# A hybrid decoder layer on one core: pinned even mix in the middle stage, and a first projection by chunks of transposed x

## The chip, the cores and the metric

The kernel runs on one core of a Trainium2 chip. The metric is the device time of one launch in microseconds (us); three runs of the kernel before are given, and their median counts.

## The reference, cut to what matters

One layer over 1024 tokens of 1024 features, all float32. One input projection feeds three groups of heads (six differential heads, six DSA heads, four retention heads) and a SiLU gate; their outputs meet in one output projection.

```python
def reference(x, ...):
    u = rms_norm(h, attn_norm)                        # per token, over 1024 features
    proj = u @ w_in                                   # 1024 x 4040 columns
    dq, dk, dv, sq, ckv, iq, ik, iw, rq, rk, rv, gate = split(proj)
    # A: softmax(q0 k0) - lam * softmax(q1 k1), causal, times dv; rms_norm per head
    o_a = diff_attention(dq, dk, dv, diff_lambda, diff_norm, lam_init)
    # B: index score = sum_h iw_h * relu(iq_h . ik); the 256 best keys of each query;
    #    softmax over those keys of the latent ckv
    o_b = dsa_attention(sq, rms_norm(ckv, kv_norm), iq, ik, iw, w_uk, w_uv, 256)
    # C: chunkwise retention on rotary q, k; rms_norm per head
    o_c = retention(rotary(rq), rotary(rk), rv, ret_norm)
    y = silu(gate) * concat(o_a, o_b, o_c)
    return rms_norm(h + y @ w_out, final_norm)
```

## The kernel before, in words

Every large product is done in split form: an operand is kept as a rounded high part and a low rest (`split`, L121 to 123: a copy into the high tile, then source minus high into the low tile), and a product is three matmuls, high-high, high-low and low-high. `uh` and `ul` are the two parts of the normed, transposed x; `wh`, `wl` and `wb` those of weights; `woh`, `wol` those of the output weights. PSUM has three kinds of tile with two buffers each: `pS` (1024 columns), `pB` and `pG` (512).

*Front.* Eight blocks of 128 tokens are loaded as rows (`x<-in_x_dram`, 512 KB each). `prep_a` (L206) squares and sums a block on ScalarE (L211), makes the reciprocal root (`rstd_small`, L193 to 204) and scales the block on VectorE (L213). `prep_b` (L215) transposes it with eight TensorE transposes (L220) and splits it into `uh` and `ul`. The weights of the differential values, index keys and index weights (456 columns, `wide` L231, `wsplit`) are split, and `gemm` of kind "a" (L282 to 284) makes eight blocks of 24 matmuls with 456 columns; `dv_evac` (L563) evicts them and transposes the index keys.

*Index stage.* The gemms iq0 and iq1 (kind "b": a unit is 48 matmuls of 512 columns, L130 to 132), then the index scores (`idx_scores`, L322: two matmuls, a Relu, a multiply and add on VectorE) mixed with iq2, iq3, q0 and k0.

*Middle stage* (L871 to 873). Three streams: the differential attention of three pairs of heads, 48 steps (`attend`, L585); the top-k and ties of blocks 3 and 2; the remaining gemm units. A step of the attention has scores on TensorE (L651), a bias, scaling and maximum for each of two softmaxes on VectorE (L662), the exponentials on ScalarE (L664), the combination on GpSimd and VectorE (L676 to 680), transposes (L611), copies by ScalarE (L113), and after every second step the products with the values (L626). `topk` (L357) finds each query's 256th best score by 31 bits: in each bit three blocks are counted on ScalarE (L392) and three on VectorE (L378), and then the cut is adapted (L397 to 399). `ties` (L416) then makes the mask of a block (L424 to 430), six blocks in all; four of them are given to the next stage in the program.

*DSA, first half* (queries 0 to 511, 24 steps: L720, 721 scores, L728 softmax, L734 and 736, L758), mixed with the ties, with `out_weights` (L894: 16 loads of w_out of 256 KB, eight split by ScalarE and VectorE and eight by GpSimd), with retention and a part of the output projection. *DSA, second half*, with retention and `project`; then the rest of `project` (L905, L935 to 937).

The order of the work comes from two places. `mix` (L46) writes the program: it takes a step from the stream that has used the least share of its weight. The Tile scheduler then orders each engine's instructions by its own estimate of when they are ready, with the program's order as priority. Only under `manual_schedule` an engine keeps the program's order: for TensorE in the index stage and within one group of L626. The weights in the middle are 36 (attention), 13 (top-k), 119 (gemms).

Of the kernel before, what the change touches and what calls it, by code (L numbers as in the profile page):

```python
# [18 lines left out]
S = 1024  # L19
D = 1024  # L20
NB = 8
# [10 lines left out]
K = {'mk': 'up ky', 'mp': 's2 g5 g4', 'rt': ('hl', 'pq'), 's0': ('gg', 'gg', 'ag', 'gg', 'vg', 'gg', 'vg', 'vg'), 'xp': 2, 'bufs': (8, 3, 3, 5, 3, 4, 1), 'pp': (7,), 'rot': 0, 'order': 'g0 g1 k1 q1 k2', 'order2': 'q2 g2 rq g6 s0 ck g7 s1 M g3 rv rk | ', 'wd': 36, 'wt': 13, 'wg': 119, 'gw': 56, 'rw': 26, 'rx': 132, 'pw': 40, 'ow': 84, 'nf': 2, 'ev': 200, 'late': 8, 'de': ('aa', 'aa', 'aa'), 'da': 'ax', 'gd': (7, 4, 2), 'hlp': 'sqkk', 'tkp': '', 'vt': 'v', 'rs': 'x', 'nv': 1, 'dn': 'v', 'ws': 'gg', 'oe': ('av', 'gg'), 'one': 0, 'idx': (42, 40), 'iqs': 'iq2 iq3 q0 k0'}  # L32
# [36 lines left out]
class Trunk:  # L69
    def __init__(self, ctx, tc, ins, out):  # L70
        self.tc, self.nc = tc, tc.nc
        self.i, self.out = ins, out
        self.sb = ctx.enter_context(tc.tile_pool(name="sb", bufs=1))
        self.ps = ctx.enter_context(tc.tile_pool(name="ps", bufs=1, space=PSUM))
        self.dr = ctx.enter_context(tc.tile_pool(name="dr", bufs=1, space=bass.MemoryType.DRAM))
        self.n = 0
        self.late = []
# [57 lines left out]
    def setup(self):  # L135
# [4 lines left out]
        self.gb = self.ptile(1024)  # L140
        nc.scalar.dma_start(self.gb, bass.AP(tensor=i["attn_norm"].tensor, offset=i["attn_norm"].offset,
                                             ap=[[0, 128], [1, 1024]]))
        self.x = {}
        for b in range(NB):
            self.x[b] = self.slot("x", [128, 1024])
            nc.sync.dma_start(self.x[b], i["x"][0, b * 128:(b + 1) * 128, :])
            if b == K["xp"] - 1:
                self.wide()
# [44 lines left out]
    def rstd_small(self, ss, n, tag):  # L193
        nc = self.nc
        w = ss.shape[1]
        t = self.sb.tile([128, 3, w], F, name=self.name("rs"), tag=tag, bufs=2)
        v, r, q = (t[:, j] for j in range(3))
        nc.vector.tensor_scalar(v, ss, 1.0 / n, EPS, op0=OP.mult, op1=OP.add)
        nc.scalar.activation(r, v, AF.Ln)
        nc.scalar.activation(r, r, AF.Exp, scale=-0.5)  # L200
        nc.vector.scalar_tensor_tensor(q, r, v, r, op0=OP.mult, op1=OP.mult)
# [4 lines left out]
    def prep_a(self, b):  # L206
        nc = self.nc
        xt = self.x[b]
        junk = self.half("junk", [128, 1024], BF)
        ss = self.sb.tile([128, 1], F, name=self.name("ss"), tag="ss", bufs=2)  # L210
        nc.scalar.activation(junk, xt, AF.Square, accum_out=ss)  # L211
        r = self.rstd_small(ss, D, "rs1")
        nc.vector.scalar_tensor_tensor(xt, xt, r, self.gb, op0=OP.mult, op1=OP.mult)  # L213

    def prep_b(self, b):  # L215
        nc = self.nc
        xt = self.x.pop(b)
        p = self.pS()
        for k in range(KC):
            nc.tensor.transpose(p[:, k * 128:(k + 1) * 128], xt[:, k * 128:(k + 1) * 128], self.ident)  # L220
        pv = p.rearrange("p (k s) -> p k s", k=KC)
        sl = slice(b * 128, (b + 1) * 128)
        self.split(self.uh[:, :, sl], self.ul[:, :, sl], pv)
# [7 lines left out]
    def wide(self):  # L231
        raws = []
        for k0 in range(0, KC, 2):
            tag, bufs = ("pq", NPQ) if k0 < 2 * NPQ else ("hl", NHL)
            raw = self.sb.tile([128, 2, WA], F, name=self.name("wr"), tag=tag, bufs=bufs)
            for a, b, c in ((0, 384, C_DV), (384, WA, C_IK)):
                self.nc.sync.dma_start(raw[:, :, a:b], self.i["w_in"][
                    0, k0 * 128:(k0 + 2) * 128, c:c + b - a].rearrange("(k p) c -> p k c", p=128))
            raws.append(raw)
        self.dvw = raws  # L240

    def wsplit(self, c0, w):
        hs, ls = [], []
        if w == WA:
# [5 lines left out]
            for k in range(KC):  # L250
                self.split(hs[k], ls[k], self.dvw[k // 2][:, k % 2], *K["s0"][k])
# [17 lines left out]
    def gemm(self, unit):  # L269
# [3 lines left out]
        for j in range(2 if kind == "b" else NB):  # L273
# [3 lines left out]
            for k in range(KC):  # L277
                uh, ul = self.uh[:, k, sl], self.ul[:, k, sl]
# [158 lines left out]
    def rms_cs(self, y, tmp, p, gain, ones):  # L437
        nc = self.nc
        sq, v, r = tmp
        nc.scalar.activation(sq, y, AF.Square)  # L440
# [18 lines left out]
    def finish(self, c, half, gain, bufs, p):  # L459
        nc = self.nc  # L460
        y, g, v, r = bufs
        hs = slice(half * 512, half * 512 + 512)
        nc.sync.dma_start(y, self.yo[c][:, hs])
        self.rms_cs(y, (g, v, r), p, self.g2[gain], self.bd)
        nc.sync.dma_start(v, self.gd[c][:, hs])
        nc.gpsimd.tensor_tensor(y, y, v, OP.mult)
        nc.sync.dma_start(self.yd[half][c], y)
# [95 lines left out]
    def dv_evac(self):  # L563
# [3 lines left out]
        self.kkh, self.kkl = self.slot("kkh", [128, S], FR), self.slot("kkl", [128, S], FR)  # L567
        kt = self.half("kt", [128, NB, 64])

        def evac(b, ps):  # L570
            nc.scalar.activation(self.v[:, b, :], ps[:, 0:384], AF.Copy)
            nc.scalar.activation(kt[:, b], ps[:, 384:448], AF.Copy)
            nc.vector.tensor_scalar(self.iw[:, b], ps[:, 448:456], IDX_SCALE, None, op0=OP.mult)
            if b % 4 == 3:
                sl = slice(b * 128 - 384, b * 128 + 128)
                p = self.pB()
                for j in range(4):
                    nc.tensor.transpose(p[0:64, j * 128:(j + 1) * 128], kt[:, b - 3 + j], self.ident)
                self.split(self.kkh[0:64, sl], self.kkl[0:64, sl], p[0:64])
            if b == NB - 1:  # L580
                self.mv(self.kkh[64:128], self.kkh[0:64])
                self.mv(self.kkl[64:128], self.kkl[0:64])
        return evac

    def attend(self, pair, stages, GB=2, groups=(3, 2, 1, 0)):  # L585
# [7 lines left out]
        hd = {}  # L593
        for t in range(N + 2):
            if t < N:
                a, g, i = steps[t]
                if a not in hd:
                    hd[a] = head(a)
                val[t] = scores(hd[a], i)
            if t >= 2:  # L600
                a, g, i = steps[t - 2]
                pr = val.pop(t - 2)
                if (g, a) not in pts:
                    pts[g, a] = self.sb.tile([128, NB, W], F, name=self.name("pt"), tag="pt", bufs=2)
                pt = pts[g, a]
                qo = (i - g * GB) * 128
                for k0 in range(0, i + 1, 4):
                    nk = min(4, i + 1 - k0)
                    p = self.pB((128, 4, 128))
                    for k in range(nk):  # L610
                        nc.tensor.transpose(p[:, k], pr[:, (k0 + k) * 128:(k0 + k + 1) * 128], self.ident)  # L611
                    self.cp(self.evac_eng[k0 // 4], pt[:, k0:k0 + nk, qo:qo + 128], p[:, :nk])
            if 0 <= t - 1 < N:
                val[t - 1] = comb(val[t - 1])
            if t < N:
                val[t] = soft(steps[t][2], val[t])
            if t >= 2 and steps[t - 2][2] % GB == GB - 1:
# [4 lines left out]
                with self.tc.manual_schedule(engines={mybir.EngineType.PE}):  # L622
# [6 lines left out]
                yield 0.5, (a, g, o)  # L629
            yield (steps[min(t, N - 1)][2] + 1) / 4.5, None  # L630

    def diff(self, pair):
# [52 lines left out]
        for cost, ev in self.attend(pair, (head, scores, soft, comb), GB):  # L685
            if ev:
                a, g, o = ev
                self.raw_store(pair, a, g, o)
                if a == 1 and g % 2 == 0:
                    self.late.append([K["late"], pair, g // 2])  # L690
# [3 lines left out]
    def tick(self, n=1):  # L694
        for e in self.late:
            e[0] -= n
        while self.late and self.late[0][0] <= 0:
            _, pair, half = self.late.pop(0)
            self.finish(pair, half, "diff_norm", [self.half("f") for _ in range(4)], self.pB())
# [67 lines left out]
    def ckv_evac(self):  # L767
# [3 lines left out]
        def evac(half, ps):  # L771
# [3 lines left out]
            self.rms_cs(ck, (sq, v, r), self.pG(), self.kvg, self.ct)  # L775
            self.split(self.ckh[:, sl], self.ckl[:, sl], ck)
# [54 lines left out]
    def run(self):  # L831
# [31 lines left out]
        for b in range(NB):  # L863
            self.prep_a(b)
            self.prep_b(b)
        drain(self.gemm(("a", C_DV, WA, self.dv_evac())))
        with self.tc.manual_schedule(engines={mybir.EngineType.PE}):
# [112 lines left out]
```

## Time and profile before

| | |
|---|---|
| median of three runs | 785.36 us (785.06, 785.36, 791.89) |
| profiled execution | 785.29 us, of which the span is 783.6 us |
| granted TensorE clock over the span | 0.974 |
| TensorE busy | 724.2 us (92%), 4314 matmuls |
| VectorE busy | 551.5 us (70%) |
| ScalarE, GpSimd busy | 447.6 us (57%), 311.5 us (40%) |

Busy time is summed over instructions of one engine; overlapping matmuls count once. The share is that of the whole span, in which the stages have different limits, so the stages are read one by one. PE is TensorE, DVE is VectorE, ACT is ScalarE, POOL is GpSimd, SP is SyncE, which issues most transfers. A granted clock of 1.00 is 2.4 GHz and 0.50 is 1.2 GHz.

### The profile page before, as it was taken

The numbers are of one execution on the slowest core, as the hardware profiler recorded it, in microseconds if no ns is written. First come the engines' busy times: TensorE is split into PE (matmuls) and PEld (weight loads), VectorE is DVE, ScalarE is ACT, GpSimd is POOL, SyncE is SP. The second block draws the span as 40 slices with busy tenths as digits, with TensorE's granted clock in tenths as the row PEclk, the third lists the DMA queues.
The fourth block names the chain that finished last, engine by engine and source line by source line (L and its number), as shares of the span: only waits on it lengthen the run. The fifth ranks groups of instructions, "written<-read, shape, count | busy, mean of one in ns | idle before, by whom it ended". The sixth has DMA issues, their size and how long they took to land.

```text
span 783.6 us, 12891 instructions
## 1 busy us (share of the span) xinstructions
PE 724.2 (92%) x4314; PEld 597.4 (76%) x4314; DVE 551.5 (70%) x1312; ACT 447.6 (57%) x989; POOL 311.5 (40%) x343
## 2 busy tenths in 40 slices
PE   3999999999999999988799789998978999999996
PEld 3798888887887898766577567997855887787884
DVE  5920277789999989999889997325657766664443
ACT  4531255559888968787755566434356656554332
POOL 6401322225434438557347699335733242120000
PEclk9999999999999999999899999999968999999999
DMA  9303645454374352461274476564578974413351
GB/s 332 78 1 71 197 136 145 139 137 132 99 218 115 85 163 78 120 169 35 67 206 144 144 215 190 158 192 160 158 213 236 281 200 127 123 48 108 118 176 59
DMA packets 93250, 113.05 MB, mean 144 GB/s; under 512 B 11904, under 2 KB 63488, under 8 KB 93056
## 3 DMA queue, kind: packets, MB, share of 16 engines
q1 hardware_dynamic: 91888, 109.61, 48.1%
q10 hardware_dynamic: 1296, 2.62, 0.9%
q8 instruction: 34, 0.56, 0.3%
q14 instruction: 32, 0.26, 0.1%
HBM read 75.50 MB, written 36.18 MB: 143 GB/s over the span
## 4 chain that ended last, share of the span: by engine, by line
PE 61%; DVE 16%; DMA 6%; issue 6%; POOL 5%; ACT 4%; SPq 0%; DVEq 0%; POOLq 0%; ACTq 0%
PE pB L626 6%; PE pG L130 6%; PE pG L132 6%; PE pG L131 5%; PE pB L611 4%; PE pG L282 4%; PE pG L936 4%; PE pG L937 4%; PE pG L935 4%; PE pG L283 4%; PE pG L284 4%; DVE jv L378 3%; DMA wr<-in_w_in_dram 2%; PE pS L344 2%; PE pS L343 2%
## 5 line engine op out<-in xcount | busy, mean ns | idle before, releaser
L130 PE MATMUL pG<-uh,wh 128*128 128x512 f32 x352 | 141.6, 402 | 1.8 <-DVE gt L827 1.8
L132 PE MATMUL pG<-uh,wl 128*128 128x512 f32 x352 | 140.7, 400 | 0.6 <-POOL wl L123 0.6
L131 PE MATMUL pG<-ul,wh 128*128 128x512 f32 x352 | 139.4, 396 | 0.0
L123 POOL TENSOR_TENSOR wl<-wr,wh 128x512 fp32r<-128x512 f32 x56 | 79.3, 1430 | 106.3 <-PE pG L131 69.4
L392 ACT ACTIVATE ja<-sc,tk_c 128x896 int8<-128x896 f32 (+2 forms) x93 | 83.2, 895 | 17.3 <-DVE tk_c L399 12.0
L113 ACT ACTIVATE pt<-pB 128x512 f32<-128x512 f32 (+2 forms) x120 | 58.8, 496 | 43.8 <-PE pB L611 43.5
L130 PEld LDWEIGHTS pG<-uh,wh 128*128 128x128 f32 x352 | 66.8, 190 | 16.4 <-DVE gt L827 2.4
L132 PEld LDWEIGHTS pG<-uh,wl 128*128 128x128 f32 x352 | 66.4, 189 | 16.1 <-POOL wl L123 0.9
L611 PE MATMUL pB<-ident,pp 128*128 128x128 f32 x432 | 72.9, 287 | 5.5 <-DVE gt L758 3.4
L626 PE MATMUL pB<-pt,v 128*64 128x128 f32 x864 | 70.8, 302 | 7.6 <-ACT pt L113 7.0
L131 PEld LDWEIGHTS pG<-ul,wh 128*128 128x128 f32 x352 | 66.7, 189 | 13.0 <-issue 0.2
L626 PEld LDWEIGHTS pB<-pt,v 128*64 128x64 f32 x864 | 57.7, 147 | 18.9 <-ACT pt L113 9.5
L378 DVE TENSOR_SCALAR_CACHE_REDUCE jv<-sc,tk_c 128x640 bf16<-128x640 f32 (+4 forms) x81 | 69.2, 855 | 1.0
L611 PEld LDWEIGHTS pB<-ident,pp 128*128 128x128 f32 x432 | 51.2, 144 | 22.2 <-issue 9.1
L677 POOL TENSOR_SCALAR pq<-pq,mx 128x896 f32<-128x896 f32 (+7 forms) x48 | 43.2, 901 | 58.6 <-DVE mx L676 55.8
L119 POOL TENSOR_SCALAR wh<-wr 128x512 fp32r<-128x512 f32 x56 | 37.8, 680 | 59.9 <-DMA wr<-in_w_in_dram 54.3
L282 PE MATMUL pG<-wh,uh 128*128 128x256 f32 x192 | 55.0, 288 | 2.6 <-POOL wh L119 2.6
L283 PE MATMUL pG<-wl,uh 128*128 128x256 f32 x192 | 54.9, 286 | 0.0
L284 PE MATMUL pG<-wh,ul 128*128 128x256 f32 x192 | 54.3, 284 | 0.0
L346 ACT ACTIVATE pp<-pS 128x1024 f32<-128x1024 f32 (+5 forms) x48 | 36.5, 760 | 31.1 <-PE pS L344 31.0
L651 PE MATMUL pS<-st,st 128*128 128x512 f32 (+3 forms) x144 | 43.3, 368 | 11.5 <-DVE mx L662 8.9
L351 DVE SCALAR_TENSOR_TENSOR sc<-pp,iw,sc 128x1024 f32<-128x1024 f32 (+5 forms) x42 | 43.5, 1044 | 14.3 <-ACT pp L346 13.6
(218 smaller groups left out, 1756.1 us busy)
## 6 DMA issues: line engine op xcount, KB each, us to landing
wr<-in_w_in_dram SPq DMA_DIRECT2D x56, 256.0 KB, 3.2
st<-qdq SPq DMA_DIRECT2D x24, 256.0 KB, 4.2
st<-qkk SPq DMA_DIRECT2D x18, 256.0 KB, 5.9
x<-in_x_dram SPq DMA_DIRECT2D x8, 512.0 KB, 6.6
qiq<-hl SPq DMA_DIRECT2D x16, 256.0 KB, 3.5
st<-qiq SPq DMA_DIRECT2D x8, 512.0 KB, 3.3
wr<-in_w_out_dram SPq DMA_DIRECT2D x16, 256.0 KB, 3.4
xr<-in_x_dram SPq DMA_DIRECT2D x8, 512.0 KB, 3.5
```

The lines of the kernel that those rows point to most:

```text
L113: self.nc.scalar.activation(out, in_, AF.Copy)
L123: (self.nc.vector if e2 == "v" else self.nc.gpsimd).tensor_tensor(lo, src, hi.bitcast(F), OP.subtract)
L130: mm(ps, wh, xh, start=start, stop=False)
L131: mm(ps, wh, xl, start=False, stop=False)
L132: mm(ps, wl, xh, start=False, stop=stop)
L282: mm(ps, uh, hs[k], start=k == 0, stop=False)
L283: mm(ps, uh, ls[k], start=False, stop=False)
L284: mm(ps, ul, hs[k], start=False, stop=k == KC - 1)
L378: nc.vector.tensor_scalar(jv[:, :nv[b]], hb if b == 7 and bit >= 16 else sc[b], t, 0.0, op0=op, op1=OP.add, accum_out=cnt[:, j:j + 1])
L392: nc.scalar.activation(ja[:, :nv[b]], sc[b], AF.Sign, bias=cut(b), scale=-1.0, accum_out=cnt[:, cols[b]:cols[b] + 1])
L611: nc.tensor.transpose(p[:, k], pr[:, (k0 + k) * 128:(k0 + k + 1) * 128], self.ident)
L626: self.last = nc.tensor.matmul(o[u * 64:(u + 1) * 64], vals[k], pts[g, a][:, k, u * 128:(u + 1) * 128], start=k == (i if u else 0), stop=k ...
```

## The change

In the front x arrives already transposed, as 16 half chunks of 128 features by 512 tokens, and the 456 weight columns arrive packed, chunk by chunk; both are laid out by the host. x is multiplied by the norm's gain and split without the row norm, and the projection runs chunk by chunk for six blocks of tokens at once, in two pS and two pB tiles. Meanwhile x is loaded a second time by rows, squared and summed; the eight reciprocal roots are spread over all partitions by eight matmuls with a matrix of ones. The evictions of the projection multiply by the row norm, and x is multiplied by it and split again for all that follows, half by half (`resplit`); blocks 6 and 7 are projected between, from the first split. The transposes of the index keys move behind iq0. TensorE, VectorE and SyncE keep the program's order in the front.

In the middle TensorE keeps the program's order, and the weights are the streams' own totals, 149.4, 86 and 233.5, so that each stream spends the same share at every point. The turn of a step (transposes and copies) stands behind a yield of its own, step costs are written anew, and the rests of the differential norms and of the latent's norm are put off by some ticks.

```diff
-K = {... 's0': ('gg', 'gg', 'ag', 'gg', 'vg', 'gg', 'vg', 'vg'), ... 'wd': 36, 'wt': 13, 'wg': 119, ... 'late': 8, ...}
+K = {... 's0': ('gg', 'ag', 'gg', 'ag', 'gg', 'ag', 'gg', 'ag'), ... 'wd': 149.4, 'wt': 86, 'wg': 233.5, ... 'late': 12, 'rest': 6, 'turn': 2.5, ...}
...
+    def split_x(self, k):
+        nc = self.nc
+        g = self.gk[:, k:k + 1]
+        for c in (slice(0, 512), slice(512, S)):
+            hi, x = self.uh[:, k, c], self.x[k][:, c]
+            nc.scalar.activation(hi, x, AF.Copy, scale=g)
+            nc.vector.scalar_tensor_tensor(self.ul[:, k, c], x, g, hi.bitcast(F), op0=OP.mult, op1=OP.subtract)
+
+    def row_rms(self):
+        nc = self.nc
+        ss = self.const("ss", [128, NB])
+        for b in range(NB):
+            row = self.ptile(D) if b % 2 else self.wtile("row", [D], F)
+            nc.sync.dma_start(row, self.i["x"][0, b * 128:(b + 1) * 128, :])
+            junk = self.half("junk", [128, D], BF)
+            nc.scalar.activation(junk, row, AF.Square, accum_out=ss[:, b:b + 1])
+        self.rn = self.rstd_small(ss, D, "rs8")
         p = self.pS()
+        for b in range(NB):
...
+            nc.vector.tensor_scalar(dg, self.ident, self.rn[:, b:b + 1], None, op0=OP.mult)
+            nc.tensor.matmul(p[:, b * 128:(b + 1) * 128], self.ct, dg, start=True, stop=True)
+        return p
+
+    def resplit(self, p, half):
+        nc = self.nc
+        c = slice(half * 512, half * 512 + 512)
+        for k in range(KC + 1):
+            if k < KC:
+                x = self.x[k][:, c]
+                nc.vector.scalar_tensor_tensor(x, x, self.gk[:, k:k + 1], p[:, c], op0=OP.mult, op1=OP.mult)
+                nc.scalar.activation(self.uh[:, k, c], x, AF.Copy)
+            if k:
+                hi = self.uh[:, k - 1, c]
+                nc.vector.tensor_tensor(self.ul[:, k - 1, c], self.x[k - 1][:, c], hi.bitcast(F), OP.subtract)
+
+    def front(self):
...
         for k in range(KC):
+            self.split_w(k)
+            self.split_x(k)
+            step(range(6), k)
+        rb = self.row_rms()
+        for b in range(6):
+            evac(b, ps[b])
+        self.resplit(rb, 0)
+        ps[6:] = [self.pG()[:, :WA] for _ in range(2)]
+        for k in range(KC):
+            step((6, 7), k)
+        for b in (6, 7):
+            evac(b, ps[b])
+        self.resplit(rb, 1)
+        return keys
...
+                while k == 4 and self.deferred:
+                    self.deferred.pop(0)()
...
+            if pinned:
+                cost = 0.5 + 0.2 * (steps[min(t, N - 1)][2] + 1)
+                yield cost, None
+                if t >= 2:
+                    turn(t)
...
-        for b in range(NB):
-            self.prep_a(b)
-            self.prep_b(b)
-        drain(self.gemm(("a", C_DV, WA, self.dv_evac())))
-        with self.tc.manual_schedule(engines={mybir.EngineType.PE}):
-            drain(units("iq0 iq1"))
+        et = mybir.EngineType
+        with self.tc.manual_schedule(engines={et.PE, et.DVE, et.SP}):
+            keys = self.front()
+        with self.tc.manual_schedule(engines={et.PE}):
+            drain(units("iq0"))
+            keys()
+            drain(units("iq1"))
...
-        interleave((seq(*(self.diff(p) for p in range(3))), K["wd"]),
-                   (seq(self.topk(), self.ties((3, 2))), K["wt"]),
-                   (units(K["order"] + " " + K["order2"].split("|")[0]), K["wg"]))
+        with self.tc.manual_schedule(engines={mybir.EngineType.PE}):
+            interleave((seq(*(self.diff(p) for p in range(3))), K["wd"]),
+                       (seq(self.topk(), self.ties((3, 2))), K["wt"]),
+                       (units(K["order"] + " " + K["order2"].split("|")[0]), K["wg"]))
```

TensorE in the front. Before, the program begins with the transposes of blocks 0 and 1 (`pS<-ident,x`), then come the three matmuls of each chunk for one block of tokens (`wb` the weights):

```order
L220 MATMUL pS_129<-ident,x_77 128x128 x8
L220 MATMUL pS_151<-ident,x_79 128x128 x8
L282 MATMUL pG_321<-wb_299,uh 128x456
L283 MATMUL pG_321<-wb_301,uh 128x456
L284 MATMUL pG_321<-wb_299,ul 128x456
```

Now the 144 matmuls of six blocks end in a pB tile, the row scale is spread into a pS tile by eight matmuls with ones (`dg<-ct`), and blocks 6 and 7 follow in pG tiles:

```order
L263 MATMUL pB_137<-wb_126,uh 128x456
L263 MATMUL pB_137<-wb_130,uh 128x456
L263 MATMUL pB_137<-wb_126,ul 128x456
L233 MATMUL pS_371<-dg_372,ct 128x128 x4
L233 MATMUL pS_371<-dg_381,ct 128x128 x4
L263 MATMUL pG_432<-wb_125,uh 128x456
L263 MATMUL pG_433<-wb_125,uh 128x456
```

The transposes are gone, and a matmul that needs a free pS tile and the row norm of all blocks stands in the middle of the front.

VectorE in the middle stage. Before, the top-k ends (`tk_w`, `tk_c`) and the first tie begins (`eq`, L425 and 426) ahead of the softmax of the 33rd differential step (`pq_3815`):

```order
L406 TENSOR_SCALAR tk_w<-tk_n 128x3
L679 TENSOR_SCALAR mx_3666<-mx_3666,nlam 128x1
L408 TENSOR_TENSOR tk_w<-tk_w 128x3
L680 SCALAR_TENSOR_TENSOR pp_3670<-pp_3670,mx_3666,pq_3667 128x256
L409 TENSOR_TENSOR tk_c<-tk_c,tk_w 128x3
L425 TENSOR_SCALAR eq_5610<-sg_5609 128x512
L426 SCALAR_TENSOR_TENSOR sc_709<-eq_5610 128x512
L662 ISA pq_3815,mx_3814<-pS_3808,cb 128x896
```

Now the last of six ties (`eq_5930`; its lines are L481 to 486) ends ahead of the softmax of the 25th step (`pq_3472`; the line is now L739):

```order
L481 TENSOR_SCALAR eq_5930<-sg_5929 128x640
L482 SCALAR_TENSOR_TENSOR sc_678<-eq_5930 128x640
L508 TENSOR_TENSOR hl_3273<-hl_3273 128x512
L483 TENSOR_SCALAR nd_5931<-nd_5931,sc_678 128x1
L484 TENSOR_SCALAR nd_5931<-nd_5931 128x1
L485 SCALAR_TENSOR_TENSOR eq_5930<-sc_678,nd_5931,sg_5929 128x640
L123 TENSOR_TENSOR ck_3272<-hl_3273,ck_3271 128x512
L486 TENSOR_SCALAR sc_677<-eq_5930 128x640
L501 TENSOR_SCALAR hl_3393<-pB_3436 128x512
L739 ISA pq_3472,mx_3471<-pS_3460,cb 128x896
```

The top-k and all ties have moved ahead by eight differential steps and more.

VectorE in the first DSA half. Before, the first split of output weights (`wol`) stands behind the last retention gemm's rotary products (L491, 492), at the tenth of the 24 DSA steps:

```order
L491 TENSOR_TENSOR rt_5396<-pG_5371,trigdec 128x256
L492 TENSOR_TENSOR rt_5396<-pG_5371,trigdec 128x256
L758 TENSOR_TENSOR gt_5850<-pB_5839,gt_5850 128x128
L123 TENSOR_TENSOR wol<-wr_5722,woh 128x512
L728 ISA pp_5909,mx_5908<-pS_5903,sc_709 128x512
```

Now the seventh and eighth stand ahead of the eleventh step's softmax (`pp_5861`; the line is now L805):

```order
L508 TENSOR_TENSOR f_5510<-f_5510,f_5511 128x512
L123 TENSOR_TENSOR wol<-wr_6012,woh 128x512
L501 TENSOR_SCALAR f_5738<-pB_5800 128x512
L123 TENSOR_TENSOR wol<-wr_6113,woh 128x512
L805 ISA pp_5861,mx_5860<-pS_5849,cb 128x256
```

All eight have moved into the last differential steps and the first part of the DSA half.

## Rows read from the trace of the kernel before

**Rows 1.** Windows by stage: stretch, us, busy us (instructions) of PE, PEld, DVE, ACT, POOL; granted clock, DMA share, GB/s.

```profile
0.00:67.10 67.10, 52.98 (x264) 47.00 (x265) 34.98 (x74) 25.89 (x58) 21.88 (x28) 0.97 0.36 120
67.10:177.40 110.30, 110.30 (x502) 91.06 (x501) 68.47 (x97) 51.39 (x78) 31.07 (x29) 1.00 0.53 149
177.40:405.70 228.30, 214.56 (x1261) 176.83 (x1260) 214.83 (x586) 183.33 (x420) 114.94 (x132) 0.98 0.44 120
...
177.40:311.75 134.35, 132.84 (x813) 111.96 (x812) 126.79 (x362) 112.63 (x255) 64.05 (x79) 1.00 0.46 128
...
405.70:559.20 153.50, 140.27 (x946) 118.82 (x946) 103.60 (x240) 75.70 (x179) 98.20 (x99) 0.98 0.57 173
559.20:594.80 35.60, 29.31 (x173) 20.41 (x171) 22.40 (x76) 19.22 (x53) 14.29 (x16) 0.76 0.72 207
594.80:783.60 188.80, 176.77 (x1175) 143.24 (x1175) 107.26 (x244) 92.11 (x203) 31.09 (x42) 0.99 0.48 145
```

**Rows 2.** Waits of PE from 178 to 520 us: total us, times, longest.

```profile
PE pS L651 <- DVE mx L662: 8.9, 5, 3.1
...
PE pB L611 <- DVE f L442: 1.0, 1, 1.0
```

**Rows 3.** Groups of DVE, 178 to 520 us: busy us, mean ns | idle before.

```profile
L378 DVE TENSOR_SCALAR_CACHE_REDUCE jv<-sc,tk_c 128x1024 bf16<-128x1024 f32 x16 | 20.4, 1276 | 0.3
L378 DVE TENSOR_SCALAR_CACHE_REDUCE jv<-hb,tk_c 128x1024 bf16<-128x1024 bf16 x13 | 16.6, 1274 | 0.2
...
L680 DVE SCALAR_TENSOR_TENSOR pp<-pp,mx,pq 128x896 f32<-128x896 f32 (+7 forms) x48 | 48.5, 1011 | 5.7 <-POOL pq L677 5.0
L662 DVE CUSTOM_DVE_ANT_0 pq<-pS,cb 128x896 f32<-128x896 f32 (+7 forms) x48 | 35.9, 748 | 3.4 <-PE pS L651 3.2
L426 DVE TENSOR_TENSOR_SCAN sc<-eq 128x512 f32<-128x512 bf16 (+5 forms) x6 | 12.6, 2103 | 0.1
L429 DVE SCALAR_TENSOR_TENSOR eq<-sc,nd,sg 128x512 bf16<-128x512 f32 (+5 forms) x6 | 7.8, 1297 | 0.0
L430 DVE TENSOR_SCALAR sc<-eq 128x512 bf16<-128x512 bf16 (+5 forms) x6 | 4.4, 732 | 0.0
L425 DVE TENSOR_SCALAR eq<-sg 128x512 bf16<-128x512 bf16 (+5 forms) x6 | 3.7, 618 | 2.7 <-ACT sg L424 2.6
```

**Rows 4.** Timeline of PE at two places: start us, us, what.

```profile
205.58 0.39 PE L132 MATMUL pG<-uh,wl 128*128 128x512 f32 x1
205.81 0.40 PE L130 MATMUL pG<-uh,wh 128*128 128x512 f32 x1
206.13 1.96 PE L626 MATMUL pB<-pt,v 128*64 128x128 f32 x30
208.03 0.65 PE L611 MATMUL pB<-ident,pp 128*128 128x128 f32 x4
208.44 0.70 PE L651 MATMUL pS<-st,st 128*128 128x512 f32 x2
...
554.76 0.28 PE L284 MATMUL pG<-wh,ul 128*128 128x256 f32 x1
554.88 0.28 PE L282 MATMUL pG<-wh,uh 128*128 128x256 f32 x1
```

**Rows 5.** Groups of the front, 0 to 68 us.

```profile
L213 DVE SCALAR_TENSOR_TENSOR x<-x,rs,pp 128x1024 f32<-128x1024 f32 x8 | 13.0, 1628 | 0.2
...
L220 PE MATMUL pS<-ident,x 128*128 128x128 f32 x64 | 10.3, 312 | 13.2 <-DVE rs L198 11.0 <-DVE x L213 2.2
```

**Rows 6.** The page's DMA issues: count, KB each, median us to landing.

```profile
x<-in_x_dram SPq DMA_DIRECT2D x8, 512.0 KB, 6.6
```

**Rows 7.** Chain that ended last, 559 to 596 us: start us, us, what.

```profile
568.38 4.43 DMA wr<-in_w_out_dram
572.84 0.64 ACT woh L113
573.50 0.69 DVE wol L123
```

More of the change, by code (lines that the diff above doesn't have):

```diff
@@ L76, in __init__ @@
         self.n = 0
-        self.late = []
+        self.late, self.deferred = [], []
         self.qd, self.gd, self.rt = {}, {}, {}
@@ new lines, in front, with step @@
+    def front(self):
+        nc = self.nc
+        hs, ls = self.wsplit(C_DV, WA)
+        evac, keys = self.dv_evac()
+        mm = nc.tensor.matmul
+        big = [self.pS(), self.pS()]
+        ps = [big[b // 2][:, b % 2 * 512:b % 2 * 512 + WA] for b in range(4)] + [self.pB()[:, :WA] for _ in range(2)]
+        ps += [None, None]
+        def step(blocks, k):
+            st, sp = k == 0, k == KC - 1
+            todo = [[(b, self.uh, hs, st, False) for b in blocks], [(b, self.uh, ls, False, False) for b in blocks],
+                    [(b, self.ul, hs, False, sp) for b in blocks]]
+            order = [t for b in zip(*todo) for t in b] if sp else [t for w in todo for t in w]
+            for b, u, w, s0, s1 in order:
+                mm(ps[b], u[:, k, b * 128:(b + 1) * 128], w[k], start=s0, stop=s1)
+        for k in range(KC):
+            self.split_w(k)
[6 more added lines that the diff above has]
+        ps[6:] = [self.pG()[:, :WA] for _ in range(2)]
+        for k in range(KC):
+            step((6, 7), k)
[3 more added lines that the diff above has]
+        return keys
@@ L593, in attend, with turn @@
         hd = {}
+        def turn(t):
+            a, g, i = steps[t - 2]
+            pr = val.pop(t - 2)
+            if (g, a) not in pts:
+                pts[g, a] = self.sb.tile([128, NB, W], F, name=self.name("pt"), tag="pt", bufs=2)
+            pt = pts[g, a]
+            qo = (i - g * GB) * 128
+            for k0 in range(0, i + 1, 4):
+                nk = min(4, i + 1 - k0)
+                p = self.pB((128, 4, 128))
+                for k in range(nk):
+                    nc.tensor.transpose(p[:, k], pr[:, (k0 + k) * 128:(k0 + k + 1) * 128], self.ident)
+                self.cp(self.evac_eng[k0 // 4], pt[:, k0:k0 + nk, qo:qo + 128], p[:, :nk])
         for t in range(N + 2):
+            cost = (steps[min(t, N - 1)][2] + 1) / 4.5
             if t < N:
@@ L598, in attend @@
                     hd[a] = head(a)
+                    if pinned:
+                        yield K["turn"], None
                 val[t] = scores(hd[a], i)
[L600 to L612, printed above, removed]
+            if not pinned and t >= 2:
+                turn(t)
             if 0 <= t - 1 < N:
@@ L628, in attend @@
                                     start=k == (i if u else 0), stop=k == i - 1, skip_group_check=True)
-                yield 0.5, (a, g, o)
-            yield (steps[min(t, N - 1)][2] + 1) / 4.5, None
+                yield 0 if pinned else 0.5, (a, g, o)
+            yield cost, None
     def diff(self, pair):
@@ L684, in diff @@
         self.evac_eng = K["de"][pair]
-        for cost, ev in self.attend(pair, (head, scores, soft, comb), GB):
+        for cost, ev in self.attend(pair, (head, scores, soft, comb), GB, pinned=True):
             if ev:
@@ L689, in diff @@
                 if a == 1 and g % 2 == 0:
[L690 removed]
+                    self.late.append([K["late"], self.finish, pair, g // 2, "diff_norm"])
             self.tick()
@@ L697, in tick @@
         while self.late and self.late[0][0] <= 0:
-            _, pair, half = self.late.pop(0)
-            self.finish(pair, half, "diff_norm", [self.half("f") for _ in range(4)], self.pB())
+            _, do, *args = self.late.pop(0)
+            do(*args)
     def dsa(self, pair, half):
```

116 lines of the change are left out of this document (61 added, 55 removed).

## The prediction

> **What bounds the kernel now.** I read first the windows of the span by stage [rows 1]. They show four regimes. In the front (0 to 67.1 us) TensorE is busy for 53.0 of 67.1 us. From 67.1 to 177.4 it is busy for all of 110.3 us: the index stage is bound by TensorE. The middle stage is two regimes: up to 405.7 us, where the softmax of the 33rd of 48 differential steps starts, VectorE is busy for 214.8 of 228.3 us (94%), while TensorE's 214.6 includes long stretches with gemm matmuls to spare; after it TensorE has 140.3 of 153.5 us and VectorE only 103.6. From 559.2 to 594.8, the bare rest of the first DSA half, no engine is full (TensorE 29.3, VectorE 22.4 of 35.6 us) and the granted clock is 0.76. From 594.8 on TensorE is again nearly full, 176.8 of 188.8 us.
>
> Next come TensorE's waits in the middle [rows 2]: its largest is for VectorE, which has yet to read a score tile. Then the groups of VectorE [rows 3]: the top-k counts, the softmax pair and the combine are what fill it. Last come prices of single matmuls by the starts of neighbours in the timeline [rows 4]: 205.81 - 205.58 = 0.23 us for 512 columns (0.205 for 456, by proportion), 0.12 for 256, (208.03 - 206.13)/30 = 0.063 for a PV matmul, (208.44 - 208.03)/4 = 0.10 for a transpose.
>
> **Front.** Removed are 64 transposes (10.3 us busy) and the idle time of 13.2 us in front of them, most of it for the row norm on VectorE, and eight scalings of 1.63 us [rows 5]. TensorE now waits only for the first half chunk of x and the first weights; x loads took 6.6 us to land [rows 6], so with issue and split it begins near 9.5 us. Then 144 matmuls at 0.205 are 29.5 us; I add 2 for the slow start, and 2 for the row scale (eight small matmuls which wait for the evictions of blocks 0 and 1, since the score tiles have two buffers; blocks 6 and 7 and iq0 are queued behind them). Blocks 6 and 7 are 48 x 0.205 = 9.8 us, to 53. Beside them VectorE re-splits half of x: 16 instructions of 512 elements at 0.69 [rows 7] to 0.81 (half of L213) are 11 to 13 us, so that iq0 starts near 54 instead of 67.1: **-13**. If nothing stalls it is -18; if the second reading of x by rows, eight loads queued on SP behind the sixteen half chunks, lands later than the 30 us that the 144 matmuls leave it, every engine waits there, and the gain may be nothing. I take -13, from the rows for matmuls, which are most of it. The key transposes only move behind iq0.
>
> **Start of the middle.** After the last index matmul 36 gemm matmuls precede the first differential scores, before it was 63: 27 x 0.23 = -6.2. For the re-split of half 1, on which the second half of iq0 waits, and the moved keys I add 1.3 (0 to 4). The first softmax of the middle, at 177.4 before, then starts at 177.4 - 13 - 6.2 + 1.3 = 159.5.
>
> **Middle, first part.** The pinned TensorE order spreads the gemms evenly, but VectorE's order is still the scheduler's: there the last top-k bit stands at step 20 or 21, and all six ties stand ahead of the softmax of step 25. So before that softmax VectorE must do what it did in 177.4 to 405.7, without eight steps, with five more ties. A step is two softmax reads of 0.748 and a combine of 1.011, 2.5 us (its short instructions overlap these) [rows 3]: -20. Six ties are 12.6 + 7.8 + 4.4 + 3.7 = 28.5, five with their short ones 25 (the first stood partly in that window already). Some four evictions and copies fall outside, -3. The sum is 214.8 - 20 + 25 - 3 = 217 us busy; at the 94% of [rows 1], **231 us**. Its lower bound is 217, at no idle time; the upper one 245, at 88%, if the pinned TensorE makes VectorE wait in turn.
>
> TensorE needs less in this part. Its order lists 477 matmuls of 512 columns (109.7), 192 of 256 (23.0), 72 of scores (12.6 by columns), 105 transposes (10.5), 216 of PV (13.6) and a few of norms (1): 171 us. The same prices for the groups recorded in 177.4 to 311.75 sum to about 128 for 134.35 us in which TensorE was busy for 132.8 [rows 1], a factor of 1.05; so 180 us. It idles for some 50 us of the first part, and because it is pinned, no later gemm fills that.
>
> **Middle, second part.** The next 24 steps have 288 x 0.23 + 384 x 0.12 + 24 x 0.17 = 116.4, with scores, transposes and PV (12.6 + 10.8 + 12.7) 152.5, by 1.05 **160 us**. VectorE has 24 x 3 us and evictions, under 100, and waits. Low bound 153, high 168. The end of the last retention gemm, 559.2 before, comes at 159.5 + 231 + 160 = 550.
>
> **First DSA half.** Before, nine of its 24 steps ran under that gemm and 15 in the 35.6 us behind it, 2.37 us a step. Now all 24 stand behind it, with the last two differential steps: 24 x 2.37 = **57**. The low bound is VectorE's busy rate, 22.4/15 x 24 = 36, with the differential tail 42. The high one is given by the weights of the output projection, whose eight VectorE splits now stand within the first twelve steps: each costs a load of 4.43, ScalarE's 0.64 and VectorE's 0.69 [rows 7], 5.8 a cycle, eight of them 46, and twelve steps at 2.37 behind them, 74. I take 57, by the window that holds the same work. The second DSA half then starts near 607.5 instead of 594.8. From there on nothing is moved: 188.8 us.
>
> **Sum.** 159.5 + 231 + 160 + 57 + 188.8 = 796.3 of span, against 783.6. The profiled execution took 1.7 us more than its span (785.29), and that is within 0.1 of the median, 785.36. So **797** us, 1.5% slower. I cost the other edits at nothing. The rests of the differential norms and of the latent, now deferred by some steps, lie beside gemm matmuls that TensorE has in hand; the one wait of TensorE for such a norm was 1.0 us [rows 2], so eight rests without that cover would be 8 us. The row-scaled evictions have the width of those before.
>
> **Two rules of the Trainium skill.** The counts of the top-k took 1276 ns from f32 and 1274 from bf16, at 1024 elements [rows 3]. The Trainium skill, "VectorE: DVE Perf Modes", section "The perf-mode tier table (the rule you actually need)", has tensor_scalar at four times the base rate from bf16 in SBUF and at twice from f32. By that the bf16 count would be far shorter than the other, and the counts about half as long, and the first part would be bound by TensorE. The trace disagrees, the two are alike, and this count writes an accumulator too; the sum goes by the rows.
>
> The windows show a part bound by VectorE and one bound by TensorE [rows 1]. "Perfetto Trace Analysis" of the Trainium skill, section "Optimization Strategy", says that interleaving regimes which differ in their most contended engine may help; that speaks for an even mix. It is the first rival below, which is priced from rows alone.
>
> **Rivals.**
> - *The even mix works (faster).* If VectorE's first part fell below TensorE's 180 us, the middle would be TensorE's 180 + 160, 51 us less: 797 - 51 = 746. For it: VectorE's 318 us of busy time in the middle [rows 1] would fit under TensorE's 340, if spread. Against it: all ties and bits are ahead of step 25, 217 us by rows, so it decides only if 37 us of them overlap or move. 0.08.
> - *VectorE packs without gaps, and the DSA half runs at VectorE's pace.* 217 instead of 231 and 42 to 50 instead of 57: 768 to 776, half of it 785. For it: waits for TensorE in [rows 3] are small, and TensorE, ahead of VectorE, would leave none. Against it: the 35.6 us window shows no pace near that. 0.25.
> - *The output weights set the DSA half.* 74 instead of 57: 814. For it: in the window before, the chain that ended last runs through one such load, its conversion and its split [rows 7]. Against it: TensorE is ahead of VectorE, and the loads are ready to issue earlier. 0.13.
> - *The front gains nothing.* 797 + 13 = 810, if rows of x or the re-split are late. For it: two readings of x and twice the elementwise passes. 0.12.
>
> **How the numbers follow.** The forecast has 0.42, with its own range of 785 to 812. One per cent, about what a measurement can tell here, is 777.5 to 793.2. Slower by more: 0.32 of the forecast's 0.42, the 0.13, and 0.10 of the 0.12, together 0.55. Faster by more: 0.08, and 0.12 of the 0.25, 0.20. The rest, 0.25, is within 1%. The range leaves out the working even mix and small tails: 768 to 814.
>
> **What would show it.** Right: iq0's first matmul at 52 to 57 us; the 25th softmax at 380 to 400 with VectorE above 90% busy until then and TensorE below 80%; TensorE full for the 160 us behind it; the DSA steps with idle on all engines and a clock below 1. Wrong: VectorE with idle over 15% in the first part, or the 25th softmax before 360 (the even mix), TensorE waiting at 40 to 60 us for the row scale (the front), or a first DSA half of 45 us or of 70.

## The result and the profile after

The changed kernel takes 860.52 us (median of four; 856.8 to 862.29) against 785.21: a ratio of 1.098, interval 1.091 to 1.105. Slower was forecast, but 797 us, with 814 as the upper end. The profiled execution took 856.8 us, its span is 855.1.

The windows by stage of the kernel after, cut at the first index gemm, the first softmax of the middle, the softmax of the 25th step, the first DSA softmax and the second DSA half (columns as in [rows 1]):

```profile
0.00:57.17 57.17, 45.38 (x208) 40.75 (x209) 32.63 (x69) 34.08 (x64) 24.79 (x29) 0.97 0.65 214
57.17:168.70 111.53, 105.77 (x479) 87.51 (x479) 76.01 (x107) 53.20 (x78) 29.04 (x26) 0.98 0.50 140
...
168.70:408.66 239.96, 198.87 (x1065) 164.01 (x1066) 218.77 (x552) 169.64 (x380) 93.80 (x109) 0.89 0.39 103
...
408.66:603.70 195.04, 169.99 (x1087) 144.36 (x1086) 95.34 (x230) 84.62 (x195) 104.64 (x120) 0.97 0.44 122
603.70:668.50 64.80, 41.41 (x255) 27.01 (x255) 39.95 (x124) 31.68 (x90) 22.63 (x22) 0.81 0.71 211
668.50:855.10 186.60, 174.99 (x1175) 142.67 (x1174) 105.95 (x240) 90.56 (x200) 26.50 (x38) 0.99 0.48 143
```

Against [rows 1]: the front is 9.9 us shorter, the tail (188.8 before) 2 shorter. All of the loss lies in the middle, 435 us. In the kernel before it runs from 177.4 to 525.1, where the first DSA softmax stands, and the first DSA half from there to 594.8:

```profile
177.40:525.10 347.70, 323.49 (x1954) 266.90 (x1953) 299.08 (x769) 248.39 (x572) 190.99 (x199) 0.98 0.49 139
...
525.14:594.81 69.67, 60.61 (x424) 49.13 (x422) 41.76 (x134) 29.82 (x81) 36.41 (x49) 0.88 0.62 186
```

The middle of the kernel after:

```profile
168.70:603.70 435.00, 368.86 (x2151) 308.37 (x2152) 314.12 (x781) 254.26 (x574) 198.44 (x229) 0.92 0.41 111
```

TensorE idles 66 us instead of 24 and is busy for 45 us more. Some 200 more matmuls stand in it, most of which the first DSA half has lost: 424 there before, 255 now, for nearly the same duration (69.7 and 64.8 us). And the granted clock is 0.92 instead of 0.98. TensorE's groups in this stretch say whom it waited for (last column):

```profile
L130 PE MATMUL pG<-uh,wh 128*128 128x512 f32 x249 | 108.6, 436 | 5.7 <-POOL wh L119 3.0 <-ACT hl L355 2.6
...
L728 PE MATMUL pS<-st,st 128*128 128x512 f32 (+3 forms) x142 | 36.0, 362 | 11.2 <-DMA st<-qdk 8.6 <-DVE mx L739 2.6
L703 PE MATMUL pB<-pt,v 128*64 128x128 f32 x412 | 33.7, 304 | 30.9 <-ACT pt L113 30.9
```

The waits of scores for VectorE, 8.9 us in [rows 2], have shrunk to 2.6. What grew is the wait of the value products (L703, L626 before) for ScalarE's copies of the transposes: 30.9 us. Before, in the view of [rows 2], it was 6.5 us:

```profile
PE pB L626 <- ACT pt L113: 6.5, 3, 2.7
```

Three such waits of the kernel after in TensorE's timeline, and ScalarE's beside the second:

```profile
203.16 1.96 PE L703 MATMUL pB<-pt,v 128*64 128x128 f32 x30 [2.48 <-ACT pt L113]
...
269.16 1.03 PE L671 MATMUL pB<-ident,pp 128*128 128x128 f32 x8
272.87 3.40 PE L703 MATMUL pB<-pt,v 128*64 128x128 f32 x30 [2.68 <-ACT pt L113]
276.20 0.68 PE L130 MATMUL pG<-uh,wh 128*128 128x512 f32 x1
...
357.30 1.96 PE L703 MATMUL pB<-pt,v 128*64 128x128 f32 x30 [1.22 <-ACT pt L113]
```

```profile
270.72 1.04 ACT L448 ACTIVATE ja<-sc,tk_c 128x896 int8<-128x896 f32 x1
271.67 0.19 ACT L448 ACTIVATION_READ_ACCUMULATOR ja<-sc,tk_c 128x1 f32 x1
271.76 1.06 ACT L113 ACTIVATE pt<-pB 128x512 f32<-128x512 f32 x2
```

The transposes end near 270.2; ScalarE has a top-k count in front of their copies; TensorE, held to its order, cannot take the gemm matmul at 276.20 meanwhile. The same 30 products then take 3.40 us, against 1.96 at 203.16 and 357.30, and the granted clock of these slices is low:

```profile
265.00:270.00 5.00, 5.00 (x28) 4.17 (x26) 4.83 (x12) 4.46 (x12) 2.15 (x2) 1.00 0.41 107
270.00:275.00 5.00, 2.32 (x25) 2.13 (x25) 4.96 (x14) 4.55 (x10) 2.54 (x4) 0.82 0.70 180
275.00:280.00 5.00, 5.00 (x27) 4.06 (x25) 4.43 (x13) 3.70 (x8) 0.00 (x0) 0.84 0.16 43
```

Here the wait is paid for twice: as idle time, and as slower matmuls behind it. It is not so after every wait. Six of the waits ahead of value products are longer than 2 us; after those of 2.68, 2.80, 2.87 and 4.27 us the products were slower than elsewhere, after those of 2.48 us (at 203.16) and 3.60 us (at 517.48) they were not, and the granted clock stayed at 1.00. What decides it stays open.

### The profile page after: what moved, and what is told of

It reads as the page before. It is cut to its first block, busy times and chain, and to the rows that moved or that the text cites. A ratio compares the mean times of both kernels' runs of the same rounds, so it can differ in the third digit from the quotient of the medians.

```text
span 855.1 us, 12844 instructions
## 1 busy us (share of the span) xinstructions
PE 736.4 (86%) x4266; PEld 606.3 (71%) x4266; DVE 568.7 (67%) x1320; ACT 463.8 (54%) x1004; POOL 301.4 (35%) x343
## 5 line engine op out<-in xcount | busy, mean ns | idle before, releaser
L130 PE MATMUL pG<-uh,wh 128*128 128x512 f32 x352 | 150.0, 426 | 8.1 <-POOL wh L119 3.0
L132 PE MATMUL pG<-uh,wl 128*128 128x512 f32 x352 | 143.6, 408 | 4.5 <-POOL wl L123 4.5
L131 PE MATMUL pG<-ul,wh 128*128 128x512 f32 x352 | 143.0, 406 | 0.0
L703 PE MATMUL pB<-pt,v 128*64 128x128 f32 x864 | 68.2, 296 | 37.9 <-ACT pt L113 32.1
L703 PEld LDWEIGHTS pB<-pt,v 128*64 128x64 f32 x864 | 55.8, 144 | 48.6 <-ACT pt L113 40.2
L130 PEld LDWEIGHTS pG<-uh,wh 128*128 128x128 f32 x352 | 69.8, 198 | 27.4 <-issue 7.1
L132 PEld LDWEIGHTS pG<-uh,wl 128*128 128x128 f32 x352 | 69.4, 197 | 22.9 <-POOL wl L123 7.0
L131 PEld LDWEIGHTS pG<-ul,wh 128*128 128x128 f32 x352 | 69.8, 198 | 12.9 <-issue 1.2
L741 ACT ACTIVATE pq<-pq,mx 128x896 f32<-128x896 f32 (+7 forms) x48 | 37.2, 774 | 67.6 <-DVE mx L739 64.2
L754 POOL TENSOR_SCALAR pq<-pq,mx 128x896 f32<-128x896 f32 (+7 forms) x48 | 36.9, 769 | 96.3 <-DVE mx L753 80.2
L739 DVE CUSTOM_DVE_ANT_0 pq<-pS,cb 128x896 f32<-128x896 f32 (+7 forms) x48 | 36.1, 753 | 39.1 <-PE pS L728 39.0
L757 DVE SCALAR_TENSOR_TENSOR pp<-pp,mx,pq 128x896 f32<-128x896 f32 (+7 forms) x48 | 47.0, 980 | 10.4 <-POOL pq L754 9.3
```

The costliest lines, as they stand in the source:

```text
L130: mm(ps, wh, xh, start=start, stop=False)
L131: mm(ps, wh, xl, start=False, stop=False)
L132: mm(ps, wl, xh, start=False, stop=stop)
L703: self.last = nc.tensor.matmul(o[u * 64:(u + 1) * 64], vals[k], pts[g, a][:, k, u * 128:(u + 1) * 128], start=k == (i if u else 0), stop=k ...
```

## The experiments

Theories: A, the pinned order puts the value products right behind their transposes; B, top-k and ties stand too early on VectorE (the forecast's); C, the front disturbs what follows; D, a fixed TensorE order stalls wherever a producer is late; E, it does so only because of the top-k's counts; G, gemms taken out of the DSA half cost what they take.

**The two halves of the change.** Front alone, with the middle of before:

> The new front with the middle stage as before (free TensorE order, old weights, no deferred rests). Theory A (the loss comes from the pinned TensorE order of the middle, which puts the value products right behind the transposes and so waits for ScalarE's copies): the front keeps the 10 us that its first index gemm is earlier (57.2 against 67.1 us), about 775 us. Theory B (the early top-k and ties, 240 us for the first 24 steps, then a part bound by TensorE): also about 775. Theory C (the new front disturbs what follows: later loads, waits for the key stacks): 785 or more.

773.87 us, ratio 0.986 (0.982 to 0.990): C falls, and this version is 1.4% faster than the kernel before. The middle alone, on the old front:

> The old front with the pinned even middle stage. Theories A and B: the whole loss and none of the front's gain, 860 + 10 = 870 us. Theory C: clearly under 850.

865.76 us, ratio 1.103 (1.100 to 1.106). The middle carries the whole loss.

**Value products later.** The last yield of a step moves ahead of the value products, directly behind `turn(t)`:

```diff
                     turn(t)
+                yield cost, None
...
-            yield cost, None
+            if not pinned:
+                yield cost, None
```

> The changed kernel, but in a differential step the value products stand behind the step's second yield, so that gemm matmuls (about 2 us on the mean) lie between the transposes and them; TensorE stays pinned. Theory A: most of the 32 us that TensorE waited for ScalarE's copies ahead of the value products go, and the clock recovers: 825 to 835 us. Theory B: the first 24 steps are bound by VectorE, so only the waits of the later part (about 10 us) are won: 848 to 855.

840.57 us, ratio 1.070 (1.066 to 1.074): 20 us are won, between A and B. TensorE's groups of this run:

```profile
L130 PE MATMUL pG<-uh,wh 128*128 128x512 f32 x249 | 106.9, 429 | 20.1 <-POOL wh L119 10.3 <-DVE gt L910 6.9 <-ACT hl L355 2.9
...
L704 PE MATMUL pB<-pt,v 128*64 128x128 f32 x412 | 30.2, 284 | 3.3 <-ACT pt L113 3.2
```

The wait for copies fell from 30.9 to 3.2 us, but now the first matmul of a gemm chunk (L130) waits 20.1 us instead of 5.7, for weight splits on GpSimd and evictions. Half of what was won there moved on to the next late producer.

**TensorE free, the new program.**

```diff
-        with self.tc.manual_schedule(engines={mybir.EngineType.PE}):
-            interleave(...)
+        interleave(...)
```

> The changed kernel's program, weights and deferred rests, but TensorE's order in the middle is left to the scheduler. There the top-k ends at the 31st step instead of the 20th. Theory A: the waits for copies go, and the front's gain stays: 775 to 790 us. Theory B: the top-k is back where it was, so the same, 775 to 790; together with the run above it tells whether the pin acts by the waits or by where VectorE's work goes. If the new program order itself is bad (costs, weights, deferral): 810 or more.

801.92 us, ratio 1.021 (1.017 to 1.025), between the two forecasts. The pin costs 58.6 us, and the new program without it another 28 beside the front alone. (The edit also frees the order within a group of value products, which the kernel before holds; and with TensorE free the scheduler orders the other engines differently too. Both are part of what is called the pin here.) Its two parts, to and from the 25th softmax, are

```profile
169.65:344.65 175.00, 167.41 (x1004) 139.45 (x1004) 166.01 (x465) 146.47 (x338) 78.80 (x96) 0.99 0.46 125
344.65:545.21 200.56, 179.57 (x1116) 147.60 (x1116) 138.31 (x315) 97.56 (x227) 126.89 (x131) 0.96 0.46 131
```

The first 24 steps take 175 us instead of 240, of which some is moved work (the pinned order has 61 matmuls more there and 29 fewer behind); from there on the pinned kernel is not slower (195 and 201).

**Even weights alone.** In the front-only kernel, at its own step costs:

```diff
-'wd': 36, 'wt': 13, 'wg': 119
+'wd': 60, 'wt': 86, 'wg': 233.5
```

> The front-only kernel (773.9 us) with the weights of the middle set to the streams' totals at its own step costs, 60, 86 and 233.5; TensorE stays free. In its order the gemms that stood in the first DSA half (35 us of matmuls) move into the last eight differential steps. Theory G (matmuls taken out of the DSA half, where they filled TensorE's idle time, cost what they take in a middle that has no such idle time): 774 + 25 to 35, about 803 us. If the placement of the gemms doesn't matter: 770 to 780.

789.78 us, ratio 1.009 (1.006 to 1.012): 16 us above the front alone, half of G's price. Its DSA half:

```profile
532.68:592.52 59.84, 43.18 (x253) 29.69 (x248) 41.34 (x124) 30.89 (x88) 26.00 (x26) 0.74 0.74 225
```

It has 171 matmuls fewer than in the front-only kernel (x424 in 64.17 us) and is only 4.3 us shorter. And with the unpinned program, `'wd': 87, 'wt': 13, 'wg': 119`:

> The unpinned kernel (801.9 us) with weights 87, 13 and 119, which give the streams about the shares of the kernel before at the new step costs; 23 of the 35 us of matmuls are back in the DSA half. Theory G: 780 to 787 us. If instead the deferred rests and the new step order cost the 28 us: 800.

796.63 us: only 5 won. So the rest of the 28 us, 12 (801.92 against 789.78, both with even weights) to 23 (796.63 against 773.87, both with about the old shares), comes with the new step order and deferred rests, which were not taken apart.

**Where VectorE's work stands.** VectorE pinned too (`engines={et.PE, et.DVE}`, `'rs': 'a'`):

> The changed kernel with VectorE pinned to the program's order in the middle as well (and the copies of raw outputs named for ScalarE), so that the mix is even on VectorE too: the last top-k bit at the 41st differential step instead of the 20th, the ties in the last steps. Theory B (top-k and ties too early on VectorE starve TensorE first and VectorE later): 815 to 830 us. Theory D (a fixed order on TensorE makes the two wait for each other wherever VectorE's work stands): 855 or more.

916.5 us, ratio 1.169 (1.162 to 1.176): what theory D expected, though the second fixed order also adds waits of its own, 47.7 us ahead of the scores instead of 11.2. The ties behind the last combine:

```diff
-(self.ties((7, 6, 5, 4)), 110),
+(self.behind(self.dlast.ins, self.ties((7, 6, 5, 4))), 110),
```

> The changed kernel with the ties of blocks 7 to 4 queued on VectorE behind the last differential combine, that is in the first DSA half, where VectorE has 25 of 65 us idle and which does not need them. Theory B (the first 24 steps are bound by VectorE's 219 us): about 20 us less, 838 to 843. If the first part is held by TensorE's order: 855 to 862.

871.27 us, ratio 1.109 (1.104 to 1.115): not faster. Windows of the first 24 steps, of pin_dve and of ties_late:

```profile
166.97:427.03 260.06, 204.37 (x1094) 167.07 (x1094) 156.28 (x411) 137.09 (x305) 97.03 (x112) 0.88 0.34 91
```

```profile
167.81:403.60 235.79, 192.03 (x1065) 158.70 (x1066) 200.29 (x528) 166.28 (x374) 90.16 (x109) 0.92 0.38 101
```

VectorE has 62 and 18 us less to do there than in the changed kernel (218.77), and the steps take 20 us longer and 4 us less. Since pin_dve has those added waits, ties_late is the cleaner test: 4 us for 18 us of work. B falls: the length of this part does not follow VectorE's load.

**Gemms back into the DSA half.**

```diff
-'order2': '... g3 rv rk | ', 'wg': 233.5
+'order2': '... g3 | rv rk', 'wg': 192.5
```

> The changed kernel (860.5 us) with two retention gemms, rv and rk, moved from the pinned middle behind the bar, into the first DSA half, where TensorE is free (41 of 65 us busy); the gemm weight is 192.5 instead of 233.5. 39 us of matmuls leave the middle. Theory G (matmuls in the DSA half fill idle time): 25 to 35 us less, 825 to 835. If the middle's length is set by something other than the amount of TensorE work in its fixed order: 850 or more. A cost against both: the splits of the output weights come later, beside the second DSA half.

847.63 us, ratio 1.078 (1.071 to 1.086), 13 won, half of what G expected. The DSA half and what follows:

```profile
562.92:645.09 82.17, 74.80 (x588) 65.73 (x587) 43.62 (x133) 33.78 (x92) 34.74 (x45) 0.96 0.61 187
645.09:846.20 201.11, 179.55 (x1171) 143.55 (x1167) 112.09 (x246) 92.00 (x204) 36.75 (x48) 0.99 0.48 144
```

The middle lost 40 us, about what its 39 us of matmuls take; 17 came back in the DSA half and 14.5 behind it, where the later weight splits may be the reason (no run tested that). Both edits together:

> The same with the value products behind the step's second yield (pv_gap, 840.6 us). If the wait for copies and the emptied DSA half are separate costs they add: 840.6 - 25 to 35 = 806 to 815 us. If they are one and the same, 825 to 840.

836.74 us, ratio 1.065 (1.058 to 1.072), 4 below pv_gap, with overlapping intervals: they don't add.

**The pin with the old shares**, 87, 13, 119:

> The changed kernel, TensorE pinned, with weights 87, 13 and 119, about the shares of before. 23 us of matmuls return to the DSA half, the top-k ends at the 24th step instead of the 20th. Beside the unpinned kernel with the same weights (796.6 us) it gives the price of the pin alone. Theory A with D (the fixed order itself): 845 to 855, 50 to 60 above that one. If the even weights were what made the pin dear: 815 or less.

850.66 us, ratio 1.085 (1.077 to 1.093). Beside unpinned_oldmix the pin costs 54 us: the even weights are not what makes it dear. With these weights 14 of the 54 us fall behind the 25th softmax (203.5 against 189.1 us).

**The pin without most of the top-k.** `for bit in range(30, 26, -1)`, pinned and free:

> The changed kernel with 4 of the top-k's 31 bits (27 bits of counts on VectorE and ScalarE are left out; the rest of the program, ties included, stands). Theory E (the pin costs because ScalarE and VectorE hold the top-k counts, in their own order, in front of the copies and softmaxes that the fixed TensorE order waits for; in the stretches without counts the pinned middle runs as fast as the free one, 195 us against 201 from step 25 on): the price of the pin beside the next run falls from 59 to under 20 us; about 740 to 760. Theory D (the fixed order is slow wherever it stands): the price stays at 40 or more; about 790.

> The same 4 bits with TensorE free (unpinned, 801.9 us with all bits). Theory E: within 20 us of the run before, 730 to 745. Theory D: 40 or more below it.

837.44 and 789.01 us, ratios 1.067 (1.061 to 1.073) and 1.007 (1.004 to 1.011): 23 and 13 us less than with all bits. In absolute terms both theories were far off: neither expected that leaving out most of the counts wins so little. The pin still costs 48 us, so E falls and D stands. The first 24 steps, pinned and free:

```profile
168.97:384.65 215.68, 190.87 (x1065) 157.55 (x1066) 130.68 (x308) 96.72 (x218) 95.64 (x109) 0.92 0.43 115
```

```profile
169.40:338.57 169.17, 166.00 (x1002) 139.12 (x1000) 118.61 (x297) 88.41 (x205) 84.23 (x97) 0.99 0.49 130
```

With 88 us less on VectorE the pinned steps are only 24 us shorter, and VectorE is then busy for 61% of the time. The 47 us that the pinned steps still take beside the free ones come with TensorE's fixed order: 25 us of idle time instead of 3, and 25 us more busy time, with 63 matmuls more and a granted clock of 0.92 instead of 0.99. The wait of the value products for ScalarE's copies stays too:

```profile
L703 PE MATMUL pB<-pt,v 128*64 128x128 f32 x390 | 32.7, 310 | 23.4 <-ACT pt L113 23.4
```

So most of the 30.9 us does not hang on the counts that were left out, though the timeline above shows one in front of the copies.

**The ties late in the front-only kernel.**

> The front-only kernel (773.9 us) with the ties of blocks 7 to 4 behind the last differential combine. In front_only VectorE is busy for 52 of 55 us in steps 33 to 40, where these ties stand; behind the last combine TensorE runs a bare gemm stretch of 23 us in which VectorE has 3 us to do. If VectorE bounds steps 33 to 40: 10 to 15 us less, 759 to 764. If not: 772 to 776.

774.06 us, ratio 0.987 (0.980 to 0.994): no change beside front_only. Steps 33 to 40 shortened from 55 to 50 us, and the stretch behind the last step grew from 23 to 28.

## Why the prediction was right and wrong

*Front.* Right: -13 was forecast, the first index gemm begins 9.9 us earlier, and the front alone brings 11.9. The three missing microseconds lie in two waits for the row-normed evictions, ahead of the row scale (a sign of being wrong that the prediction named) and of iq0, 5.3 us where 2 were booked:

```profile
41.24 3.58 PE L233 MATMUL pS<-dg,ct 128*128 128x128 f32 x16 [2.87 <-DVE iw L636]
...
57.17 0.47 PE L130 MATMUL pG<-uh,wh 128*128 128x512 f32 x1 [2.40 <-DVE iw L636]
...
167.58 1.09 PE L728 MATMUL pS<-st,st 128*128 128x512 f32 x2 [4.75 <-DMA st<-qdk]
```

*Start of the middle.* 159.5 was forecast, 168.7 measured: the 3.2 us above, and most of the rest is the wait in the last row. The gemm matmuls between index stage and first scores, whose loss was booked as a gain of 6.2, had covered the load of the key stack; before, the first scores followed them without a wait. With TensorE free, in unpinned, the first softmax comes no earlier (169.65). A removed cover was taken for removed work.

*First part.* 231 was forecast and 240 measured, and VectorE's work there, forecast as 217 us, measured 218.8. Yet the step failed. "So before that softmax VectorE must do what it did" makes VectorE the bound; ties_late and bits4_pin, with 18 and 88 us less on VectorE, shortened the part by only 4 and 24. The number came near by luck: with that load mostly gone, in bits4_pin, the pinned order still takes 216 us. The reading behind it was open from the start. In [rows 1] TensorE is busy for 214.56 and VectorE for 214.83 of the same 228.30 us, 94% each, and the prediction set TensorE's share aside as matmuls "to spare". With TensorE free, in bits4_free, 47 us less on VectorE than in unpinned shortened the first 24 steps by only 6 (175.00 to 169.17), with TensorE busy for 166.00 of them. The kernel before itself was not tested so.

*Second part.* This is the term of the sum that failed most: "by 1.05 **160 us**", with TensorE full. It measured 195: 170.0 us busy and 25 idle, 35 of the 58.8 us by which the sum was short. The kernel before already needed 180 us for its last 24 steps, 19 of them idle:

```profile
345.27:525.14 179.87, 161.03 (x975) 131.42 (x974) 140.77 (x328) 109.69 (x254) 108.64 (x101) 0.96 0.50 147
```

At that pace the 1087 matmuls of the new order take 200 us, an estimate from these two rows that takes the matmuls as alike. So the term was too small before any pin. The unpinned kernel needs 201, so with the even weights the pin is not the cause; the waits are spread over copies, splits and evictions, and a sum of matmul prices has no place for them.

*TensorE's price.* "A factor of 1.05; so 180 us" and 160 behind it are 340 us busy; 368.9 were measured. That is 29 of the 44 us by which the middle is longer than the forecast's 231 and 160; the other 15 are idle time, 66 us instead of the 51 that the forecast implies. The factor came from a stretch in which the scheduler had chosen the order, at a clock of 1.00. A pinned order has to be priced by its neighbours: in the new order the value products stand directly behind their transposes (30.9 us of waits), and [rows 2] show only what an order with filler between leaves over. The busy time agrees with the clock: the free program's 346.9 us at 0.97 would be 366 at 0.92, an estimate near the 368.9; no run changed the clock alone.

*Its signs.* VectorE was above 90% busy up to the 25th softmax, as forecast, but that softmax came at 408.7 instead of 380 to 400, TensorE was busy for 83% until then instead of under 80%, and for 87% behind it instead of all the time.

*DSA half.* 57 was forecast, from 42 to 74, and 64.8 measured, 2.70 us a step instead of 2.37. The kind of limit was right (no engine full, a clock of 0.81), the size 7.8 short; the eight loads of output weights in a row, 74, were not reached. That gemms had filled idle time there and would cost in the middle was in the sum.

*Rest.* 188.8 forecast, 186.6 measured.

*Rivals.* The even mix, 746, fell: even weights cost 16 us with TensorE free. They also move matmuls out of the DSA half, so the two are not told apart. The Trainium skill ("Perfetto Trace Analysis", section "Optimization Strategy") says that interleaving regimes may help; these runs show no gain from it. The rival on VectorE, 217 us and 42 to 50, and that on the output weights, 74, fell with their windows (240 and 64.8 us), and front_only rules out the last. A rival with the fixed order's stalls was missing.

*Sum.* 9.2 at the start, 9 in the first part, 35 in the second, 7.8 in the DSA half, less 2.2 in the tail: 58.8, the distance from 796.3 to 855.1. By the runs, in the order in which the parts were added: -12 for the front, +16 for even weights, +12 for the rest of the program, +59 for the pin.

*Open.* After pv_gap, 39 of the pin's 59 us are not put down to single causes; part of the idle time moved to splits, evictions and loads. The step order and the deferred rests weren't tried apart.

## What to carry to other kernels

When an engine is pinned, read its new order pair by pair: an instruction directly behind the one that feeds it through another engine waits for the whole round trip, and nothing fills it (30.9 us here). Prices taken from a schedule that was free to fill need not hold for one that isn't: the same program took 59 us more. Before filler is taken out of a stage, see what else sets that stage: here a stage with idle time on all engines lost 171 matmuls and shrank by 4.3 us.

## What the runs showed that was not expected

A TensorE wait of 2.68 us was followed by matmuls at about half speed (30 products in 3.40 us instead of 1.96, slices at a granted clock of 0.82 and 0.84), while one of 3.60 us was followed by the same products in 1.96 us. And 88 us less work on VectorE, in steps where it had been busy for 91% of the time, shortened them by only 24: an engine that looks full need not set the pace.
